# The last projection of a hybrid encoder layer, computed as seven half-size block products instead of eight

## The chip, the cores and the metric

The kernel runs on one core of one Trainium2 chip. The metric is the device time of one execution in microseconds (us). A core has a matrix engine (TensorE; its rows are marked PE, and its weight loads PEld), a vector engine (DVE), an activation engine (ACT) and a general engine (POOL). Each works through its own list of instructions in order, and they wait for each other by semaphores. Transfers between memory and the on-chip buffer are issued here by a fifth engine, SyncE (SP), which also takes its list in order. Matrix products are written into eight PSUM banks; POOL cannot read those, DVE and ACT can.

## The reference

The layer normalises x (512 tokens by 1024 channels), makes one wide input projection, runs two token mixers (a chunked mLSTM and stick-breaking attention), and ends with three projections of 1024 by 1024:

```python
g_m, g_s = split(sigmoid(gates))
merged = g_m * (y_m @ w_proj_m) + g_s * (y_s @ w_proj_s)     # 512 x 1024
x = x + merged @ w_out                                       # 512 x 1024
```

The change concerns the last line only, and what prepares it. All data are float32.

## The kernel before

**Products of split numbers.** Every float32 operand is split into a rounded high part and the rest: `split` (L89 to L91) is one ACT copy for the high part and one DVE subtraction for the low part, which needs the high part. `mm3` (L84 to L87) then makes a product of three matmuls: high by high, high by low, low by high.

**Units.** The dense work is a list of 112 units, and a loop over them (L980) writes the instruction lists of all engines. A unit has a 512 KB block of a weight matrix, loaded by SP into a buffer `stg` (three of them), split into `wh` and `wl` (three of each), and 24 matmuls, each with a moving operand of 512 columns. In step c of the loop the order is: the evacuation of unit c-1 (what DVE and ACT do with its finished PSUM banks), then whatever the table `later` holds for step c, then `ahead(c)` (L973), which issues the split of unit c+2 and the load of unit c+4, then the first half of unit c's matmuls, the steps of the token mixers, and the second half. The order is fixed by hand (`manual_schedule`), so an instruction in an engine's list starts only after those written before it.

**The end of the list.** Units 88 to 95 are the projection of y_s, 96 to 103 the projection of y_m, 104 to 111 the last projection. In the first two a unit makes 128 channels for all 512 tokens; `pm_evac` (L848) evacuates a unit of the y_m projection: `gm = ps * gm` and `gm = gm + gs` on DVE, and a split of gm into `mgh` and `mgl`, the stationary operands of the last projection. The last projection (`tok_group`, L134) goes through two halves of 512 output columns; for each, four units of 256 rows of `w_out` are accumulated into four PSUM banks, one for each block of 128 tokens. After the fourth unit the banks are added to the residual `xr` on DVE, and the sums are stored (L874 to L879). The eight loads of `xr` stand in `later` at unit 104 (L962).

POOL has nothing to do in these last units.

Of the kernel before, what the change touches and what calls it, by code (L numbers as in the profile page):

```python
# [8 lines left out]
F32 = mybir.dt.float32  # L9
FR = mybir.dt.float32r  # L10
BF = mybir.dt.bfloat16
AF = mybir.ActivationFunctionType
OP = mybir.AluOpType

D = 1024
T = 512
KT = 8
TB = 4
# [16 lines left out]
def tile_hybrid_layer(  # L35
# [16 lines left out]
    nc = tc.nc  # L52
    xf = x.flatten_outer_dims()
    of = out.flatten_outer_dims()

    def pool(name, bufs=1, **k):
        return ctx.enter_context(tc.tile_pool(name=name, bufs=bufs, **k))

    cst = pool("cst")
    hp = pool("hp")  # L60
    sp = pool("sp")
    mp = pool("mp")
# [5 lines left out]
    BUFS = {"stg": 3, "wh": 3, "wl": 3, "tmp": 2, "acc": 1, "om": 3, "P5": 2, "A": 4,  # L68
            "qk": 18, "vh": 5, "vl": 5, "y": 16, "brow": 1}
# [3 lines left out]
    def blk(tag, dt=F32, shape=(512,), name=None, p=128):  # L73

        where = mp if tag in MISC else sp
        return where.tile([p] + list(shape), dt, name=name or tag, tag=tag, bufs=BUFS[tag])

    def dense_ps():
        return psd.tile([128, 512], F32, name="dps", tag="dps")
# [4 lines left out]
    def mm3(ps, ah, al, bh, bl, first, last):  # L84
        nc.tensor.matmul(ps, ah, bh, start=first, stop=False)  # L85
        nc.tensor.matmul(ps, ah, bl, start=False, stop=False)  # L86
        nc.tensor.matmul(ps, al, bh, start=False, stop=last)  # L87

    def split(src, hi, lo):  # L89
        nc.scalar.activation(hi, src, AF.Copy)  # L90
        nc.vector.tensor_tensor(lo, src, hi.bitcast(F32), op=OP.subtract)  # L91


    class Unit:


        def __init__(self, src, c0, rows=None):
            if rows is None:
                self.ap = src[:, c0:c0 + 128].rearrange("(k p) c -> p k c", p=128)
                self.shape = [KT, 128]  # L100
            else:
                self.ap = src[rows:rows + 256, c0:c0 + 512].rearrange("(k p) c -> p k c", p=128)
                self.shape = [2, 512]
            self.slow = None
            self.heavy = False

        def load(self, tag="stg"):
            self.st = blk(tag, shape=self.shape)
            nc.sync.dma_start(self.st, self.ap)
# [6 lines left out]
    units = []  # L116

    def chan_group(src, c0, n, mov, evac, slow=None):
        for ct in range(n // 128):
            u = Unit(src, c0 + 128 * ct)  # L120

            def mm(half, u=u, ct=ct):
                if half == 0:
                    u.ps = dense_ps()
                for k in range(4 * half, 4 * half + 4):
                    mh, ml = mov(k)
                    mm3(u.ps, u.wh[:, k, :], u.wl[:, k, :], mh, ml, k == 0, k == KT - 1)

            u.mm = mm
            u.evac = lambda u=u, ct=ct: evac(ct, u.ps)  # L130
            u.slow = slow
            units.append(u)

    def tok_group(src, c0, sta, evac, first=False, b0=None, row=None):  # L134
        ps = [None] * TB
        n0 = len(units)

        def evacs(ps):
            rest = None
            for tb in range(TB):  # L140
                then = evac(tb, ps[tb])
                if rest:
                    rest()
                rest = then
            if rest:
                rest()

        if row is not None:
            later.setdefault(n0 + (0 if first else 2), []).append(lambda: row.append(bias_row(b0)))
        if first:  # L150
            for tb in range(TB):
                u = Unit(src, c0, 256 * tb)
                u.evac = lambda tb=tb: evac(tb, f_ps[tb])
                units.append(u)
            return
        for g in range(4):
            u = Unit(src, c0, 256 * g)

            def mm(half, u=u, g=g):
                for tb in (2 * half, 2 * half + 1):  # L160
                    if g == 0:
                        ps[tb] = dense_ps()
                    for i in range(2):
                        k = 2 * g + i
                        sh, sl = sta(k, tb)
                        mm3(ps[tb], sh, sl, u.wh[:, i, :], u.wl[:, i, :], k == 0, k == KT - 1)

            u.mm = mm
            u.heavy = g == 3
            u.evac = (lambda: evacs(ps)) if g == 3 else (lambda: None)  # L170
            units.append(u)
# [8 lines left out]
    later = {}  # L180
# [75 lines left out]
    hh = hp.tile([128, KT, T], FR, name="hh", tag="hh")  # L256
    hl = hp.tile([128, KT, T], FR, name="hl", tag="hl")
# [37 lines left out]
    def bias_row(c0):  # L295
        b = blk("brow")
        nc.sync.dma_start(b, bass.AP(tensor=b_in.tensor, offset=b_in.offset + c0, ap=[[0, 128], [1, 512]]))
        return b
# [485 lines left out]
    gs_t, gm_t = [], []  # L784
# [42 lines left out]
    def y_late(src, dst, k, at):  # L827
        def run():
            if not big:
                y_big()  # L830
            dst[k] = big["h"][:, at, :], big["l"][:, at, :]
            split_y(src, dst, k)
        return run

    def y_own(k):
        def run():
            ymp[k] = blk("y", FR, name="ymh"), blk("y", FR, name="yml")
            split_y(y_m, ymp, k)
        return run
# [4 lines left out]
    chan_group(w_proj_s, 0, D, lambda k: ysp[k], ps_evac)  # L844

    merged = []

    def pm_evac(ct, ps):  # L848
        g, t = gs_t[ct], gm_t[ct]
        nc.vector.tensor_tensor(t, ps, t, op=OP.mult)  # L850
        nc.vector.tensor_tensor(t, t, g, op=OP.add)
        th = blk("y", FR, name="mgh")
        tl = blk("qk", FR, name="mgl")
        split(t, th, tl)
        merged.append((th, tl))

    chan_group(w_proj_m, 0, D, lambda k: ymp[k], pm_evac)
    n_proj = len(units)

    def m_sta(k, tb):  # L860
        ts = slice(tb * 128, (tb + 1) * 128)
        return merged[k][0][:, ts], merged[k][1][:, ts]

    xr = {}

    def load_xr(g):
        def run():
            xr[g] = [blk("vl" if g else "vh", shape=(512 if g else 576,), name="xr")[:, 0:512] for tb in range(TB)]
            for tb in range(TB):
                nc.sync.dma_start(xr[g][tb], xf[tb * 128:(tb + 1) * 128, g * 512:(g + 1) * 512])  # L870
        return run

    for g in range(2):
        def evac(tb, ps, g=g):  # L874
            t = xr[g][tb]
            n = 256 if g == 1 and tb == TB - 1 else 512
            for c in range(0, 512, n):
                nc.vector.tensor_tensor(t[:, c:c + n], ps[:, c:c + n], t[:, c:c + n], op=OP.add)
                nc.sync.dma_start(of[tb * 128:(tb + 1) * 128, g * 512 + c:g * 512 + c + n], t[:, c:c + n])  # L879

        tok_group(w_out, g * 512, m_sta, evac)


    f_w = []
# [74 lines left out]
    for k in range(8):  # L959
        later.setdefault(n_gates + 3 + k // 2, []).append(  # L960
            y_late(y_m, ymp, k, k) if k < 5 else y_own(k))
    later.setdefault(n_proj, []).append(load_xr(0))  # L962
    later.setdefault(n_proj, []).append(load_xr(1))

    N = len(units)
    count = {"loaded": 4, "ready": 4}
# [13 lines left out]
    for c in range(N):  # L980
# [24 lines left out]
        for e in list(pend):  # L1005
            if c >= e[0] and e[2]():
                pend.remove(e)
                g = e[3]()
# [36 lines left out]
```

## Time and profile before

| what | value |
|---|---|
| median of 3 runs | 719.03 us (718.92 to 719.14) |
| the profiled execution, its own time | 720.13 us |
| its span, from first to last instruction | 718.4 us |
| granted TensorE clock, mean | 0.997 |
| PE busy | 709.8 us (99%) |
| DVE, ACT, POOL busy | 424.5, 315.8, 93.5 us |
| bytes moved | 67.8 MB, 94 GB/s |

How to read it: a row of the timeline gives the start (us from the span's start), the duration, the engine, the line of the kernel, the operation, output and inputs by name, shapes, and a count where rows were merged; square brackets give the idle time in front and what ended it. A row of a list of groups gives a count, then the sum of busy time and the mean of one in ns. A row of a table by stretches gives the busy time of PE, PEld, DVE, ACT and POOL in each stretch with the number of instructions, then the granted clock, the share of the DMA engines and GB/s.

### The profile page before, as it was taken

How to read it: one execution, taken by the hardware profiler on the slowest of the kernel's cores; microseconds unless marked ns; L12 is line 12 of the kernel's file. 1: busy time of each engine (PE TensorE's matmuls, PEld its weight loads, DVE VectorE, ACT ScalarE, POOL GpSimd, SP SyncE). 2: the span in 40 equal slices, each digit the busy share in tenths (PEclk: the TensorE clock that was granted, in tenths of full speed). 3: DMA queues.
4: the chain of work that ended last, by engine and by line, in shares of the span. 5: the costliest groups of instructions: out<-in, count | busy, mean ns of one | idle time of the engine just before them, and what ended most of it. 6: DMA issues, size and time to landing. Idle time of an engine off the chain costs nothing.

```text
span 718.4 us, 9058 instructions
## 1 busy us (share of the span) xinstructions
PE 709.8 (99%) x3356; PEld 593.1 (83%) x3356; DVE 424.5 (59%) x663; ACT 315.8 (44%) x601; POOL 93.5 (13%) x235
## 2 busy tenths in 40 slices
PE   7999999999999999999999999999999999999997
PEld 5888888888888888888888888888888888888886
DVE  5837886656487568279944737994343254556441
ACT  5245364476255544244475534447554343222210
POOL 5422022253022112000001110000112000000000
PEclk9999999999999999999999999999999999999999
DMA  6433332233323222333332233333223333333621
GB/s 239 133 103 81 109 86 77 69 95 92 99 62 87 58 86 62 102 91 97 101 94 59 63 99 88 91 100 89 74 59 89 89 91 97 104 88 89 234 89 58
DMA packets 91475, 67.80 MB, mean 94 GB/s; under 512 B 3470, under 2 KB 77608, under 8 KB 91432
## 3 DMA queue, kind: packets, MB, share of 16 engines
q1 hardware_dynamic: 91432, 67.23, 32.8%
q8 instruction: 26, 0.43, 0.2%
q14 instruction: 17, 0.14, 0.1%
HBM read 65.12 MB, written 2.10 MB: 94 GB/s over the span
## 4 chain that ended last, share of the span: by engine, by line
PE 97%; DMA 1%; DVE 1%; POOL 0%; SPq 0%; issue 0%; ACT 0%; DVEq 0%
PE dps L85 28%; PE dps L87 27%; PE dps L86 27%; PE aps L86 2%; PE aps L87 2%; PE aps L85 2%; PE aps L440 1%; PE aps L382 1%; DMA stg<-in_w_in_dram 1%; PE dps L934 1%; PE dps L932 1%; PE dps L933 1%; PE aps L735 1%; PE aps L736 1%; PE aps L737 1%; DVE fl L891 0%
## 5 line engine op out<-in xcount | busy, mean ns | idle before, releaser
L91 DVE TENSOR_TENSOR wl<-stg,wh 128x1024 fp32r<-128x1024 f32 x108 | 132.3, 1225 | 140.3 <-ACT wh L90 139.9
L85 PE MATMUL dps<-hh,wh 128*128 128x512 f32 x448 | 175.8, 392 | 0.0
L86 PE MATMUL dps<-hl,wh 128*128 128x512 f32 x448 | 174.6, 390 | 0.0
L87 PE MATMUL dps<-hh,wl 128*128 128x512 f32 x448 | 174.6, 390 | 0.0
L90 ACT ACTIVATE wh<-stg 128x1024 fp32r<-128x1024 f32 x108 | 113.6, 1052 | 95.3 <-PE dps L87 58.6
L87 PEld LDWEIGHTS dps<-hh,wl 128*128 128x128 f32 x448 | 84.1, 188 | 17.7
L85 PEld LDWEIGHTS dps<-hh,wh 128*128 128x128 f32 x448 | 84.2, 188 | 17.5 <-issue 1.0
L86 PEld LDWEIGHTS dps<-hl,wh 128*128 128x128 f32 x448 | 84.2, 188 | 16.6
L85 PE MATMUL dps<-wh,hh 128*128 128x512 f32 x224 | 88.3, 394 | 0.0
L87 PE MATMUL dps<-wh,hl 128*128 128x512 f32 x224 | 87.4, 390 | 0.0
L86 PE MATMUL dps<-wl,hh 128*128 128x512 f32 x224 | 87.4, 390 | 0.0
L87 PEld LDWEIGHTS dps<-wh,hl 128*128 128x128 f32 x224 | 42.1, 188 | 8.9
L86 PEld LDWEIGHTS dps<-wl,hh 128*128 128x128 f32 x224 | 42.1, 188 | 8.2
L85 PEld LDWEIGHTS dps<-wh,hh 128*128 128x128 f32 x224 | 42.1, 188 | 8.2
L626 DVE SCALAR_TENSOR_TENSOR acc<-tmp,vec,acc 128x511 f32<-128x511 f32 (+2 forms) x48 | 36.0, 750 | 1.7
L629 ACT ACTIVATE tmp<-acc 128x512 f32<-128x512 f32 x16 | 10.1, 633 | 50.2 <-DVE acc L626 50.2
L415 DVE TENSOR_TENSOR_SCAN om<-om 128x512 f32<-128x512 f32 (+3 forms) x32 | 27.9, 871 | 6.3 <-POOL om L409 6.3
L409 POOL TENSOR_SCALAR_AFFINE_SELECT om<-om 128x128 f32<-128x128 f32 x32 | 12.1, 378 | 134.5 <-ACT om L407 134.5
L90 ACT ACTIVATE at_split<-aps 128x384 fp32r<-128x384 f32 (+1 forms) x24 | 11.8, 525 | 36.8 <-PE aps L440 36.8
L688 POOL TENSOR_SCALAR_AFFINE_SELECT w_all<-om 128x128 f32<-128x128 f32 x16 | 4.1, 293 | 168.9 <-DVE om L683 168.9
L91 DVE TENSOR_TENSOR at_split<-aps,at_split 128x384 fp32r<-128x384 f32 (+1 forms) x24 | 13.7, 599 | 19.8 <-ACT at_split L90 19.8
L86 PE MATMUL dps<-wl,mgh 128*128 128x512 f32 x64 | 24.9, 389 | 0.0
(239 smaller groups left out, 1170.6 us busy)
## 6 DMA issues: line engine op xcount, KB each, us to landing
stg<-in_w_in_dram SPq DMA_DIRECT2D x87, 512.0 KB, 3.7
stg<-in_w_proj_s_dram SPq DMA_DIRECT2D x8, 512.0 KB, 3.7
stg<-in_w_proj_m_dram SPq DMA_DIRECT2D x8, 512.0 KB, 3.6
stg<-in_w_out_dram SPq DMA_DIRECT2D x8, 512.0 KB, 3.7
brow<-in_b_in_dram SPq DMA_DIRECT2D x8, 256.0 KB, 4.2
xr<-in_x_dram SPq DMA_DIRECT2D x8, 256.0 KB, 5.7
out_dram<-xr SPq DMA_DIRECT2D x7, 256.0 KB, 2.3
x<-in_x_dram SPq DMA_DIRECT2D x3, 512.0 KB
```

Of the source, the lines that this page charges most:

```text
L85: nc.tensor.matmul(ps, ah, bh, start=first, stop=False)
L86: nc.tensor.matmul(ps, ah, bl, start=False, stop=False)
L87: nc.tensor.matmul(ps, al, bh, start=False, stop=last)
L90: nc.scalar.activation(hi, src, AF.Copy)
L91: nc.vector.tensor_tensor(lo, src, hi.bitcast(F32), op=OP.subtract)
L382: nc.tensor.transpose(tp[:, tb * 128:(tb + 1) * 128], self.raw[name][tb][:, hs], ident)
L409: nc.gpsimd.affine_select(out=om[:, ts], in_=om[:, ts], compare_op=OP.is_gt, fill=1.0, base=0, channel_multiplier=1, pattern=[[-1, 128]])
L415: nc.vector.tensor_tensor_scan(back, back, back, 1.0, op0=OP.mult, op1=OP.bypass)
L440: nc.tensor.transpose(tp[:, at + (i - j) * 128:at + (i - j + 1) * 128], a_t[i][:, j * 128:(j + 1) * 128], ident)
L626: nc.vector.scalar_tensor_tensor(acc[:, j:], t[:, 0:T - j], cw(3 - j, ch), acc[:, j:], op0=OP.mult, op1=OP.add)
L629: nc.scalar.activation(t, acc, AF.Sigmoid)
L735: nc.tensor.matmul(nm[:, 0:258], ph, vh, start=j == 0, stop=False)
```

## The change

The 512 tokens, 1024 inner channels and 1024 output columns are each cut in half: merged becomes A11, A12 (the first 256 tokens; channel tiles 0 to 3 and 4 to 7) and A21, A22 (the last 256 tokens), and w_out becomes B11, B12, B21, B22. Eight products of such blocks give the result; Winograd's form of Strassen's method needs seven, of sums of blocks:

- S1 = A21 + A22, S2 = S1 - A11, S3 = A11 - A21, S4 = A12 - S2
- T3 = B22 - B12, T2 = B11 + T3, T1 = B22 - T2, T4 = B21 - T2 (the sign taken up in the sums)
- P1 = A11 B11, P2 = A12 B21, P5 = S1 T1, P6 = S2 T2, P7 = S3 T3, P4 = A22 T4, P3 = S4 B22
- the four blocks of the result are sums of these: U = P1 + P6, then U + P7, and so on

A product is two new units (`Product`, g = 0 and 1) of 12 matmuls each, so the eight units 104 to 111 become fourteen, 104 to 117, in the order P1, P2, P6, P5, P7, P4, P3. Beside the matmuls:

- **S1 and S2** are made in `pm_evac` for channel tiles 4 to 7 (steps 101 to 104): two DVE additions of 128x256 and a split of the 128x512 result, behind the split of gm.
- **S3 and S4** (`s34_turn`) are made in steps 105 to 108, one channel tile a step: two DVE subtractions of 128x256 and a split.
- **T1 to T4** are made on POOL, two instructions of 128x1024 each: T3 in steps 100 and 101, T2 in 103 and 104, T1 in 105 and 106, T4 in 107 and 108.
- **Loads**: B22 in steps 96 and 97 and B12 in 98 and 99, by entries of `later`; B11 and B21 with their units; `xr` in step 102.
- **Evacuation**: each product is added to the sums it belongs to when its second unit is done. Those of P1, P2, P5, P4 and P3 are DVE additions that read PSUM (P1 with two ACT copies beside them), P6 and P7 have two such DVE additions and two and four POOL additions of 128x512.

The diff (lines of the old `load_xr` and `m_sta` left out):

```diff
--- before.py
+++ after.py
@@ -844,6 +844,7 @@
     chan_group(w_proj_s, 0, D, lambda k: ysp[k], ps_evac)
 
     merged = []
+    s12 = []
 
     def pm_evac(ct, ps):
         g, t = gs_t[ct], gm_t[ct]
@@ -853,32 +854,176 @@
         tl = blk("qk", FR, name="mgl")
         split(t, th, tl)
         merged.append((th, tl))
+        if ct >= 4:
+            a = gm_t[ct - 4]
+            nc.vector.tensor_tensor(g[:, 0:256], a[:, 256:512], t[:, 256:512], op=OP.add)
+            nc.vector.tensor_tensor(g[:, 256:512], g[:, 0:256], a[:, 0:256], op=OP.subtract)
+            sh, sl = blk("vh", FR, (576,), name="s12h")[:, 0:512], blk("vl", FR, name="s12l")
+            split(g, sh, sl)
+            s12.append((sh, sl))
 
     chan_group(w_proj_m, 0, D, lambda k: ymp[k], pm_evac)
     n_proj = len(units)
 
...
+    s34 = []
+    raw = {}
+    def s34_turn(j):
+        a, t, g = gm_t[j], gm_t[4 + j], gs_t[4 + j]
+        if not s34:
+            s34.append(hp.tile([128, 8, T], FR, name="s34", tag="hh"))
+        nc.vector.tensor_tensor(a[:, 0:256], a[:, 0:256], a[:, 256:512], op=OP.subtract)
+        nc.vector.tensor_tensor(a[:, 256:512], t[:, 0:256], g[:, 256:512], op=OP.subtract)
+        split(a, s34[0][:, j, :], s34[0][:, 4 + j, :])
+    def w_load(name, g, tag):
+        r, c = {"B11": (0, 0), "B12": (0, 512), "B21": (512, 0), "B22": (512, 512)}[name]
+        where = mp if tag == "stg" else sp
+        t = where.tile([128, 2, 512], F32, name=name, tag=tag, bufs=BUFS[tag])
+        nc.sync.dma_start(t, w_out[r + 256 * g:r + 256 * g + 256, c:c + 512].rearrange("(k p) c -> p k c", p=128))
+        raw[name, g] = t
+    def t3(g):
+        d = raw["T3", g] = raw["B12", g]
+        nc.gpsimd.tensor_tensor(d, raw["B22", g], d, op=OP.subtract)
+    def t2(g):
+        d = raw["T2", g] = raw["B11", g]
+        nc.gpsimd.tensor_tensor(d, raw["T3", g], d, op=OP.add)
+    def t1(g):
+        if g == 0:
+            raw["t1"] = hp.tile([128, 4, 512], F32, name="t1", tag="hl")
+        d = raw["T1", g] = raw["t1"][:, 2 * g:2 * g + 2, :]
+        nc.gpsimd.tensor_tensor(d, raw["B22", g], raw["T2", g], op=OP.subtract)
+    def t4(g):
+        d = raw["T4", g] = raw["B21", g]
+        nc.gpsimd.tensor_tensor(d, d, raw["T2", g], op=OP.subtract)
+    def a_sta(k0, t0):
+        return lambda k, tb: [m[:, t0 + 128 * tb:t0 + 128 * tb + 128] for m in merged[k0 + k]]
+    def s_sta(which):
+        o = 256 * ((which - 1) % 2)
+        def sta(k, tb):
+            c = slice(o + 128 * tb, o + 128 * tb + 128)
+            if which <= 2:
+                return s12[k][0][:, c], s12[k][1][:, c]
+            return s34[0][:, k, c], s34[0][:, 4 + k, c]
+        return sta
 
     xr = {}
 
...
+    def load_xr():
+        for n, (g, tb) in enumerate([(0, 0), (0, 1), (1, 0), (1, 1), (1, 2), (1, 3), (0, 2), (0, 3)]):
+            tag = ["om", "om", "om", "acc", "tmp", "tmp", "brow", "vh"][n]
+            t = blk(tag, shape=({"om": 516, "vh": 576}.get(tag, 512),), name="xr")[:, 0:512]
+            nc.sync.dma_start(t, xf[tb * 128:(tb + 1) * 128, g * 512:(g + 1) * 512])
+            xr[g, tb] = t
+    bank = {}
+    class Product:
+        def __init__(self, p, sta, name, g, ps, tag=None, evac=None):
+            self.p, self.sta, self.name, self.g, self.ps, self.tag = p, sta, name, g, ps, tag
+            self.slow = None
+            self.heavy = False
+            self.evac = evac if g else lambda: None
+        def load(self):
+            if self.tag:
+                w_load(self.name, self.g, self.tag)
+        def split(self):
+            self.wh = blk("wh", FR, (2, 512))
+            self.wl = blk("wl", FR, (2, 512))
+            split(raw[self.name, self.g], self.wh, self.wl)
+        def mm(self, tb):
+            if self.g == 0:
+                bank[self.p, tb] = self.ps()
+            for i in range(2):
+                k = 2 * self.g + i
+                sh, sl = self.sta(k, tb)
+                mm3(bank[self.p, tb], sh, sl, self.wh[:, i, :], self.wl[:, i, :], k == 0, k == 3)
+    def add(g, tb, src, store=False, eng=None, n=512):
+        t = xr[g, tb]
+        for c in range(0, 512, n):
+            (eng or nc.vector).tensor_tensor(t[:, c:c + n], src[:, c:c + n], t[:, c:c + n], op=OP.add)
+            if store:
+                nc.sync.dma_start(of[tb * 128:(tb + 1) * 128, g * 512 + c:g * 512 + c + n], t[:, c:c + n])
+    u = []
+    def p1():
+        uu = blk("stg", shape=(2, 512), name="u")
+        for tb in range(2):
+            u.append(uu[:, tb, :])
+            nc.scalar.activation(u[tb], bank[1, tb], AF.Copy)
+            add(0, tb, bank[1, tb])
+    def p2():
+        for tb in range(2):
+            add(0, tb, bank[2, tb], True)
+    def p6():
+        for tb in range(2):
+            nc.vector.tensor_tensor(u[tb], u[tb], bank[6, tb], op=OP.add)
+            add(1, tb, u[tb], eng=nc.gpsimd)
+    def p5():
+        for tb in range(2):
+            add(1, 2 + tb, bank[5, tb])
+            add(1, tb, bank[5, tb])
+    def p7():
+        for tb in range(2):
+            nc.vector.tensor_tensor(u[tb], u[tb], bank[7, tb], op=OP.add)
+            add(0, 2 + tb, u[tb], eng=nc.gpsimd)
+        for tb in range(2):
+            add(1, 2 + tb, u[tb], True, nc.gpsimd)
+    def p4():
+        for tb in range(2):
+            add(0, 2 + tb, bank[4, tb], True)
+    def p3():
+        for tb in range(2):
+            add(1, tb, bank[3, tb], True, n=256 if tb else 512)
+    for p, sta, name, ps, tag, evac in (
+            (1, a_sta(0, 0), "B11", dense_ps, "A", p1),
+            (2, a_sta(4, 0), "B21", dense_ps, "stg", p2),
+            (6, s_sta(2), "T2", att_ps, None, p6),
+            (5, s_sta(1), "T1", att_ps, None, p5),
+            (7, s_sta(3), "T3", dense_ps, None, p7),
+            (4, a_sta(4, 256), "T4", dense_ps, None, p4),
+            (3, s_sta(4), "B22", att_ps, None, p3)):
+        for g in range(2):
+            units.append(Product(p, sta, name, g, ps, tag, evac))
+    def at(c, fn, *a):
+        later.setdefault(n_proj + c, []).append(lambda: fn(*a))
 
     for g in range(2):
-        def evac(tb, ps, g=g):
-            t = xr[g][tb]
-            n = 256 if g == 1 and tb == TB - 1 else 512
-            for c in range(0, 512, n):
-                nc.vector.tensor_tensor(t[:, c:c + n], ps[:, c:c + n], t[:, c:c + n], op=OP.add)
-                nc.sync.dma_start(of[tb * 128:(tb + 1) * 128, g * 512 + c:g * 512 + c + n], t[:, c:c + n])
-
-        tok_group(w_out, g * 512, m_sta, evac)
+        at(-8 + g, w_load, "B22", g, "P5")
+        at(-6 + g, w_load, "B12", g, "A")
+        at(-4 + g, t3, g)
+        at(-1 + g, t2, g)
+        at(1 + g, t1, g)
+        at(3 + g, t4, g)
+    at(-2, load_xr)
+    for j in range(4):
+        at(1 + j, s34_turn, j)
 
 
     f_w = []
@@ -959,8 +1104,6 @@
     for k in range(8):
         later.setdefault(n_gates + 3 + k // 2, []).append(
             y_late(y_m, ymp, k, k) if k < 5 else y_own(k))
-    later.setdefault(n_proj, []).append(load_xr(0))
-    later.setdefault(n_proj, []).append(load_xr(1))
 
     N = len(units)
     count = {"loaded": 4, "ready": 4}
```

More of the change, by code (lines that the diff above doesn't have):

```diff
@@ L855, in pm_evac @@
         merged.append((th, tl))
+        if ct >= 4:
[5 more added lines that the diff above has]
+            s12.append((sh, sl))
     chan_group(w_proj_m, 0, D, lambda k: ymp[k], pm_evac)
     n_proj = len(units)
-    def m_sta(k, tb):
-        ts = slice(tb * 128, (tb + 1) * 128)
-        return merged[k][0][:, ts], merged[k][1][:, ts]
@@ L864, in tile_hybrid_layer @@
-    xr = {}
[L866 to L871, printed above, removed]
-    for g in range(2):
-        def evac(tb, ps, g=g):
-            t = xr[g][tb]
-            n = 256 if g == 1 and tb == TB - 1 else 512
-            for c in range(0, 512, n):
-                nc.vector.tensor_tensor(t[:, c:c + n], ps[:, c:c + n], t[:, c:c + n], op=OP.add)
-                nc.sync.dma_start(of[tb * 128:(tb + 1) * 128, g * 512 + c:g * 512 + c + n], t[:, c:c + n])
-        tok_group(w_out, g * 512, m_sta, evac)
+    s34 = []
```

## The prediction

> **What bounds the kernel now.** I read the page's busy times and its chain of waits first, then the timeline of the matmuls at the end, then a table by stretches of the last stage.
>
> ```profile
> span 718.4 us, 9058 instructions
> PE 709.8 (99%) x3356; PEld 593.1 (83%) x3356; DVE 424.5 (59%) x663; ACT 315.8 (44%) x601; POOL 93.5 (13%) x235
> PE 97%; DMA 1%; DVE 1%; POOL 0%; SPq 0%; issue 0%; ACT 0%; DVEq 0%
> ...
> L86 PE MATMUL dps<-wl,mgh 128*128 128x512 f32 x64 | 24.9, 389 | 0.0
> ...
> 670.48 0.39 PE L85 MATMUL dps<-wh,mgh 128*128 128x512 f32 x1
> ...
> 713.77 0.39 PE L87 MATMUL dps<-wh,mgl 128*128 128x512 f32 x1
> ...
> 670.48:692.24 21.76, 21.76 (x97) 18.03 (x96) 8.87 (x10) 4.76 (x5) 0.00 (x0) 1.00 0.48 164
> ```
>
> PE is the bound, 97% of the chain. The last projection has three groups of 64 matmuls (one row shown, the other two are alike), from 670.48 to the last start at 713.77: 191 spacings in 43.29 us, **0.2267 us a matmul** (the 389 ns of a row overlap the next). A unit of 24 takes 5.44 us, and the stage would end at 714.00. No gap is left, so only fewer matmuls help, and any new wait costs in full. DVE's 59% is an average; what the change asks of DVE falls into steps 101 to 109, and a share says little of a list that is taken in order.
>
> **The matmuls removed.** Seven products of 24 are 168 instead of 192, all again with 512 moving columns: 24 x 0.2267 = **5.44 us less** on PE. A new unit of 12 lasts 2.72 us, and this is the crux: each still needs a split of 128x1024, so the time in which a split must be ready is halved in the very steps in which S1 to S4 are added to the same lists.
>
> **What DVE and ACT do in one step.** The evacuation in step 101 (unit 100's), as it is now, with the rows that give spacings:
>
> ```profile
> 654.36 0.69 DVE L850 TENSOR_TENSOR gm<-dps,gm 128x512 f32<-128x512 f32 x1 [1.15 <-PE dps L87]
> 655.09 0.69 DVE L851 TENSOR_TENSOR gm<-gm,gs 128x512 f32<-128x512 f32 x1
> 655.81 0.63 ACT L90 ACTIVATE mgh<-gm 128x512 fp32r<-128x512 f32 x1 [3.86 <-DVE gm L851]
> 656.35 1.04 ACT L90 ACTIVATE wh<-stg 128x1024 fp32r<-128x1024 f32 x1
> 656.48 0.69 DVE L91 TENSOR_TENSOR mgl<-gm,mgh 128x512 fp32r<-128x512 f32 x1 [0.70 <-ACT mgh L90]
> 657.42 1.23 DVE L91 TENSOR_TENSOR wl<-stg,wh 128x1024 fp32r<-128x1024 f32 x1 [0.26 <-ACT wh L90]
> ...
> 688.09 1.23 DVE L91 TENSOR_TENSOR wl<-stg,wh 128x1024 fp32r<-128x1024 f32 x1 [4.17 <-ACT wh L90]
> 689.24 1.28 DVE L878 TENSOR_TENSOR xr<-dps,xr 128x512 f32<-128x512 f32 x2
> ...
> 714.20 0.76 DVE L878 TENSOR_TENSOR xr<-dps,xr 128x256 f32<-128x256 f32 x2 [0.67 <-PE dps L87]
> ```
>
> From them: an independent 512 operation starts 0.60 after the one before (1.28 - 0.69, rounded), one behind a 1024 operation 1.15 (689.24 - 688.09), a 256 one lasts 0.42 and takes 0.34 when it follows another; an engine that waits for the other goes on 0.04 later. Now a step needs 3.06 + 1.23 = 4.3 us of the 5.44.
>
> *Steps 101 to 104, with S1 and S2.* mgl starts at +2.12; first addition +2.72; second, which needs it, +3.17 to +3.59; ACT's high part of S2's tile +3.63 to +4.26; its low part on DVE +4.30; ACT's wh, next in its list, +4.17; wl 1.07 later at +5.24; the next step's first operation at +5.24 + 1.15 = **+6.40**. That is over 5.44.
>
> *s34_turn and a split.* Two subtractions at 0 and +0.34 (to +0.76), ACT +0.80, its wh +1.34, wl +2.41, next +3.56: **3.56**. *Two PSUM additions* (P1, P2): **1.20**.
>
> DVE's list without any other delay, on the old trace's clock: step 101 at 654.36, 102 at 660.76, 103 at 667.16, 104 at 673.56, 105 at 679.96; 106 at 683.52 (3.56); 107 at 688.28 (1.20 + 3.56); 108 at 691.84; there wl of unit 110 starts at 691.84 + 1.20 + 2.41 = 695.45 and ends at 696.68. PE could have started unit 110 at 670.48 + 6 x 2.72 = 686.80. Its second matmul is the first that reads wl, so it starts effectively at 696.72 - 0.23 = 696.49: **9.7 us of waiting**, over units 106 to 110. From step 109 on DVE has two splits and at most four PSUM additions (2.3 + 2.4 us) in a pair of units of 5.44, and catches up. So 8 x 2.72 = 21.76 us later, at 718.25, the matmuls end, against 714.00: **+4.3 us**, or 9.7 - 5.4.
>
> **POOL beside DVE.** The trace has POOL's two-input operation only at the start, in 128x512:
>
> ```profile
> 9.83 0.68 DVE L288 TENSOR_TENSOR hh<-aps,nw_t 128x512 fp32r<-128x512 f32 x1
> 10.00 2.51 POOL L891 TENSOR_TENSOR fl<-stg,fh 128x512 fp32r<-128x512 f32 x2 [3.96 <-ACT fh L890]
> ...
> 13.76 1.62 POOL L891 TENSOR_TENSOR fl<-P,fh 128x512 fp32r<-128x512 f32 x1 [0.33 <-ACT fh L890]
> 14.14 1.79 DVE L891 TENSOR_TENSOR fl<-stg,fh 128x512 fp32r<-128x512 f32 x1
> ...
> 13.76 3.32 POOL L891 TENSOR_TENSOR fl<-P,fh 128x512 fp32r<-128x512 f32 x2 [0.33 <-ACT fh L890]
> 14.14 3.49 DVE L891 TENSOR_TENSOR fl<-stg,fh 128x512 fp32r<-128x512 f32 x2
> ...
> L891 POOL TENSOR_TENSOR fl<-stg,fh 128x512 fp32r<-128x512 f32 x2 | 2.5, 1274 | 4.0 <-ACT fh L890 4.0
> L747 POOL TENSOR_TENSOR hst<-hst 128x1 f32<-128x1 f32 x16 | 3.3, 209 | 1.3
> ```
>
> At 10.00 POOL ran beside DVE operations that read PSUM: 1274 ns each, DVE's 0.68 unharmed. From 13.76 both engines ran operations with two SBUF inputs, and took turns: DVE's first, 0.69 in the undisturbed row at 655.09, lasted 1.79, from 14.14 to 0.55 after POOL's ended at 15.38; POOL's second ended at 17.08, DVE's second at 17.63, 0.55 behind again. The one that comes second waits for nearly the whole of the other. The rest of the argument takes that for 128x1024 too, where no row shows it.
>
> A POOL operation of 1024: 0.21 + 2 x (1.274 - 0.21) = **2.34** (estimate; bounds 2 x 1.06 = 2.13 and 2 x 1.274 = 2.55). T3 (steps 100, 101) has data early and meets a DVE with 1.1 us a step to spare. The six others fall into DVE's tight stretch. T2 overwrites B11, so it starts when the split of unit 104 (then 105) is done, at the end of step 102 (103): the evacuation's multiplication reads PSUM and goes on, gm + gs, due 0.60 later, waits 1.65, twice. T1's two follow at once in step 104 and hold mgl for 1.44 (the rest of the 2.34 lies in the wait for ACT) and the first S addition for 2.24. T4 overwrites B21 behind the splits of 106 and 107: it holds the second subtraction of step 105 for 2.24, and in step 106, beside P1's two PSUM additions, the next subtraction for 1.16. Sum 1.65 + 1.65 + 1.44 + 2.24 + 2.24 + 1.16 = **10.4 us**, all in front of unit 110's split, hence all on PE. With the bounds for one operation 9.0 to 11.6; if the turn-taking covers only half of an operation of 1024, about 5.
>
> The Trainium skill, SBUF — State Buffer, Who interferes with whom, says the same against this change: an operation of DVE with two SBUF inputs and one of GpSimd (POOL) that reads SBUF exclude each other, and the earlier keeps the port for its whole instruction, whatever its length; by it the 10.4 stand and the 5 does not. GPSIMD Engine Reference, Elementwise — side-by-side cycle accounting, gives 4497 ns for 2048 elements, an estimate of 2.25 for 1024; by it the sum would be some 0.5 us lower.
>
> **The rest, costed at nothing.**
>
> ```profile
> stg<-in_w_out_dram SPq DMA_DIRECT2D x8, 512.0 KB, 3.7
> xr<-in_x_dram SPq DMA_DIRECT2D x8, 256.0 KB, 5.7
> ...
> 664.58 4.06 SPq L870 DMA_DIRECT2D xr<-in_x_dram  x8
> ```
>
> w_out is still eight loads of 512 KB. B22 and B12 stand on SP ahead of the loads of units 100 to 102, B21's load behind eight issues for xr (4.06 us); a load lands 3.7 to 5.7 us after its issue and is wanted two steps, 10.9 us, after. Without that cover B12 would land a step late, and T3 would hold step 101's additions: +1.7. P1's two ACT copies (about 0.7 each) run while ACT waits for DVE. The POOL additions of P6 and P7 come when DVE is ahead. The end is as before: one store of 256 KB, then two of half the size, 718.4 - 714.0 = 4.4 us behind the last matmul.
>
> **Sum.** -5.4 + 9.7 + 10.4 = +14.7. On the profiled execution's 720.13 that is 734.8; this execution stands 1.1 us over the median, so I forecast **733.7** for the median, from 719.03.
>
> **Rivals.**
>
> *The engines work side by side* (chance 0.15). POOL's operations don't hold DVE's, or for a part only. For it: nothing at 1024; against it the rows at 13.76. It leaves +4.3, **723.3**, or up to 728 with half holds.
>
> *DVE keeps up* (0.10), the other side: **713.6**, 719.03 - 5.44. The mechanism: splits run two units ahead, so a late DVE costs nothing until the lead is used up. It decides where wl of unit 110 is ready by 686.80. For it: DVE's busy share, 8.87 of 21.76 us; against it, the list above misses by 9.7 even without POOL. It would need step 101's chain to be shorter than 5.44, or the order in the lists to be other than written. Half of such a gain, no change at all, gets 0.04.
>
> *The clock drops* (0.13). Under my sum PE waits some 9 us before unit 106.
>
> ```profile
> 10.00:15.00 5.00, 4.34 (x12) 3.42 (x13) 4.90 (x12) 4.45 (x8) 4.50 (x5) 0.66 0.85 301
> ...
> 717.00:718.40 1.40, 0.00 (x0) 0.00 (x0) 0.00 (x0) 0.00 (x0) 0.00 (x0) 0.62 0.00 0
> ```
>
> Idle since 714, PE shows a mean granted clock of 0.62 in the last 1.4 us; between 10 and 15 us a mean of 0.66 in five, a loss of 0.34 x 5 = 1.7 us of matmul time. A drop behind the long wait meets units 106 and 107, where PE waits for DVE anyway; it costs something only if one falls on the dense run from unit 110: 733.7 + 1.7 = **735.4**. Against it: the waits before 107 to 110 come out at 1 to 3 us each, with matmuls between them. The Trainium skill, TensorE: Matmul & The Clock Gate, Part 1: The HAM clock gate, puts the drop to half speed at one idle window of about 3.4 us and the return at as long a busy one; by it the 9 us wait drops the clock, and the shorter ones don't. The last rows of the trace agree: the clock falls some 3.3 us behind the last matmul.
>
> **How the numbers follow.** Chances: my sum 0.58, the clock 0.13, side by side 0.15, keeping up 0.10, no change 0.04. Predicted is the likeliest, 733.7. The sum's own range is 732.3 to 736.6 (the bounds of POOL's operation, -1.4 and +1.2, and T3 late, +1.7). The range of 722.8 to 737.5 adds the side-by-side case below and the clock above; only the faster and unchanged cases, 0.14, and a little at the ends lie outside. A run of this kernel tells a change of 0.2%, 1.4 us, from none: faster 0.10, same 0.04, slower 0.86.
>
> **What would show it.** In the changed profile: 168 matmuls in the last projection at 0.227 us; step 101's wl about 5.2 us behind its gm multiplication and step 102's multiplication 6.4 behind that; DVE's gm + gs in steps 103 and 104 at 2.3 us instead of 0.69 while POOL runs; PE idle before units 105 to 110, most before 106, its releaser ACT's wh or DVE's wl, and none after unit 111. A DVE row of 0.69 beside a POOL operation of 2.3 would make the middle term wrong; a PE without gaps from 670 on, all of it.

## The result

The changed kernel takes 736.3 us (median of four runs, 735.1 to 737.2) where the kernel before takes 719.1: a ratio of 1.024, with a 95% interval of 1.0226 to 1.0255. It is 17.2 us slower; 14.7 were forecast, 733.7 us, with a range of 722.8 to 737.5. The profiled execution took 736.70 us, with a span of 735.0.

The page of the changed kernel, its busy times and chain of waits, and then what PE waited for (us in total, times, longest):

```profile
span 735.0 us, 9091 instructions
PE 711.6 (97%) x3332; PEld 591.4 (80%) x3332; DVE 463.5 (63%) x701; ACT 327.5 (45%) x617; POOL 124.6 (17%) x249
PE 93%; DVE 3%; DMA 1%; ACT 1%; issue 1%; POOL 0%; SPq 0%; DVEq 0%; ACTq 0%
...
PE dps L85 <- ACT wh L90: 8.8, 2, 6.2
PE aps L85 <- ACT wh L90: 2.2, 2, 2.0
PE dps L86 <- DVE wl L91: 1.6, 3, 0.8
PE aps L86 <- DVE wl L91: 1.5, 2, 0.8
```

24 matmuls fewer (3332 for 3356), and yet a longer span. PE, which had no gap in this stage, now stands 14.1 us, always for the split of a weight block. Of the 16.6 us between the two spans that and the 5.4 saved leave 7.9. Of these, 5.8 are longer spacings between matmuls with no wait between them, most at a lower clock, while the next split was not ready yet (last section); the rest lies beside the waits, where a matmul alone takes 0.5 to 0.8 us instead of the 0.227 of a dense row of them.

Where the splits are held up is in the timeline of DVE and POOL. Lines 851 and 852 are the two gm operations of `pm_evac`, 860 and 861 the additions for S1 and S2, 880 and 881 those for S3 and S4, 897, 903 and 907 are T2, T1 and T4 on POOL:

```profile
654.45 0.69 DVE L851 TENSOR_TENSOR gm<-dps,gm 128x512 f32<-128x512 f32 x1 [1.15 <-PE dps L87]
659.70 1.23 DVE L91 TENSOR_TENSOR wl<-stg,wh 128x1024 fp32r<-128x1024 f32 x1 [0.26 <-ACT wh L90]
660.85 0.68 DVE L851 TENSOR_TENSOR gm<-dps,gm 128x512 f32<-128x512 f32 x1
667.95 2.44 DVE L852 TENSOR_TENSOR gm<-gm,gs 128x512 f32<-128x512 f32 x1
672.88 0.69 DVE L91 TENSOR_TENSOR mgl<-gm,mgh 128x512 fp32r<-128x512 f32 x1 [2.49 <-PE dps L87]
677.15 0.68 DVE L851 TENSOR_TENSOR gm<-dps,gm 128x512 f32<-128x512 f32 x1
677.87 2.42 DVE L852 TENSOR_TENSOR gm<-gm,gs 128x512 f32<-128x512 f32 x1
680.99 2.08 DVE L91 TENSOR_TENSOR mgl<-gm,mgh 128x512 fp32r<-128x512 f32 x1 [0.70 <-ACT mgh L90]
682.99 2.55 DVE L860 TENSOR_TENSOR gs<-gm 128x256 f32<-128x256 f32 x1
689.24 2.47 DVE L881 TENSOR_TENSOR gm<-gm,gs 128x256 f32<-128x256 f32 x1
695.70 1.65 DVE L880 TENSOR_TENSOR gm<-gm 128x256 f32<-128x256 f32 x1
707.98 2.36 DVE L91 TENSOR_TENSOR wl<-t,wh 128x1024 fp32r<-128x1024 f32 x2 [0.25 <-ACT wh L90]
...
667.45 2.40 POOL L897 TENSOR_TENSOR B<-B,B 128x1024 f32<-128x1024 f32 x1 [20.19 <-DVE wl L91]
677.37 2.37 POOL L897 TENSOR_TENSOR B<-B,B 128x1024 f32<-128x1024 f32 x1 [7.53 <-issue]
679.70 5.57 POOL L903 TENSOR_TENSOR t<-B,B 128x1024 f32<-128x1024 f32 x2
688.95 2.48 POOL L907 TENSOR_TENSOR B<-B,B 128x1024 f32<-128x1024 f32 x1 [3.69 <-DVE wl L91]
694.66 2.40 POOL L907 TENSOR_TENSOR B<-B,B 128x1024 f32<-128x1024 f32 x1 [3.23 <-DVE wl L91]
```

Three things are to be seen. The first three rows give the chain of step 101: wl 5.25 us behind the gm multiplication, the next step's multiplication 6.40 behind it, which is more than the 5.44 of a unit. Then, each time POOL has an operation under way, one DVE operation of 0.69 or 0.42 lasts 1.65 to 2.55, and ends 0.3 to 0.6 us behind POOL's. And at 672.88 DVE comes out of a wait that PE ended: that one was not in the forecast. Everything behind it in DVE's list, up to unit 110's wl at 707.98, is later by it.

### The profile page after: what moved, and what is told of

It is laid out like the page before. It is cut to its first block, busy times and chain, and to the rows that moved or that the text cites. A ratio compares the mean times of both kernels' runs of the same rounds, so it can differ in the third digit from the quotient of the medians.

```text
span 735.0 us, 9091 instructions
## 1 busy us (share of the span) xinstructions
PE 711.6 (97%) x3332; PEld 591.4 (80%) x3332; DVE 463.5 (63%) x701; ACT 327.5 (45%) x617; POOL 124.6 (17%) x249
## 3 DMA queue, kind: packets, MB, share of 16 engines
HBM read 65.12 MB, written 2.10 MB: 91 GB/s over the span
## 4 chain that ended last, share of the span: by engine, by line
PE 93%; DVE 3%; DMA 1%; ACT 1%; issue 1%; POOL 0%; SPq 0%; DVEq 0%; ACTq 0%
PE dps L85 25%; PE dps L87 25%; PE dps L86 25%; PE aps L86 3%; PE aps L87 3%; PE aps L85 3%; PE aps L440 1%; PE aps L382 1%; DMA stg<-in_w_in_dram 1%; PE dps L1079 1%; DVE wl L91 1%; PE dps L1077 1%; PE dps L1078 1%; ACT wh L90 1%; PE aps L735 1%; PE aps L736 1%
## 5 line engine op out<-in xcount | busy, mean ns | idle before, releaser
L91 DVE TENSOR_TENSOR wl<-stg,wh 128x1024 fp32r<-128x1024 f32 x100 | 124.4, 1244 | 123.9 <-ACT wh L90 123.8
L90 ACT ACTIVATE wh<-stg 128x1024 fp32r<-128x1024 f32 x100 | 105.2, 1052 | 75.4 <-PE dps L87 41.2
L85 PE MATMUL dps<-yh,wh 128*128 128x512 f32 x64 | 24.9, 389 | 0.0
```

## The experiments

The kernel before was run beside each group: 719.06 us beside the first four, 719.39 beside the last four.

| kernel | time, us | ratio to the kernel before, 95% |
|---|---|---|
| changed kernel | 736.29 | 1.0226 to 1.0255 |
| without T1 to T4 | 726.96 | 1.0100 to 1.0134 |
| mgl of two tiles in other buffers | 733.50 | 1.0189 to 1.0219 |
| both | 723.18 | 1.0049 to 1.0080 |
| T1 to T4 as memsets | 728.67 | 1.0114 to 1.0144 |
| without any sums | 713.22 | 0.9900 to 0.9930 |
| without T1 to T4, new order | 713.61 | 0.9907 to 0.9940 |
| T1 to T4 on POOL, new order | 724.25 | 1.0055 to 1.0086 |
| T1 to T4 by ACT and DMA, new order | 714.03 | 0.9913 to 0.9943 |

A whole execution also holds what comes ahead of step 101, where these edits change nothing but T3, and that differs by over a microsecond from one profiled execution to another (see the end of the next section). Within the stage the profiles compare closely. The table has, for the changed kernel and the four runs in the old order with S1 to S4, the start of step 101's gm multiplication, the start of unit 110's wl, the time between the two, and the time from there to the end of the span, all in us. The prediction's list puts 41.1 between the two without POOL (695.45 - 654.36), and 51.5 with its 10.4.

| kernel | step 101 | wl of unit 110 | between | to the end |
|---|---|---|---|---|
| changed kernel | 654.45 | 707.98 | 53.5 | 27.0 |
| without T1 to T4 | 652.98 | 697.98 | 45.0 | 27.0 |
| mgl of two tiles in other buffers | 653.18 | 704.91 | 51.7 | 27.0 |
| both | 653.22 | 694.69 | 41.5 | 28.6 |
| T1 to T4 as memsets | 653.39 | 698.39 | 45.0 | 28.6 |

### Without T1 to T4

```diff
-        d = raw["T2", g] = raw["B11", g]
-        nc.gpsimd.tensor_tensor(d, raw["T3", g], d, op=OP.add)
+        raw["T2", g] = raw["B11", g]
...
```

(and the same for T1, T3 and T4)

> T1 to T4 are left out: POOL's eight operations of 128x1024 are gone and P6, P5, P7 and P4 take the raw blocks B11, B22, B12 and B21 in their place (the sums differ, all other work is the same). Theory: POOL's operations hold DVE's operations with two SBUF inputs, and DVE's list sets when unit 110 can start. Then DVE's rows lose their waits: gm + gs in steps 103 and 104 at 0.69 us instead of 2.44 and 2.42, and wl of unit 110 starts 8.9 us earlier (699.0 instead of 707.98, counted on from step 104 at 677.15, which stays because mgl of step 103 still waits for PE until 672.88). Time 727.4. Rival, DVE's list is long by itself and POOL costs nothing: 736.3.

726.96 us. DVE's steps 103 and 104 in this kernel:

```profile
666.48 0.69 DVE L852 TENSOR_TENSOR gm<-gm,gs 128x512 f32<-128x512 f32 x1
671.41 0.69 DVE L91 TENSOR_TENSOR mgl<-gm,mgh 128x512 fp32r<-128x512 f32 x1 [4.23 <-PE dps L87]
676.40 0.69 DVE L852 TENSOR_TENSOR gm<-gm,gs 128x512 f32<-128x512 f32 x1
```

Without POOL's operations the rows are at 0.69 again, and 9.3 us are gone, of the 8.9 expected. Within the stage it is 8.5 (53.5 - 45.0), which is what the five holds behind step 103 add up to by the changed kernel's rows (1.73 + 1.39 + 2.13 + 2.05 + 1.23). The wait that PE ends has grown from 2.49 to 4.23: its end is fixed by PE, so what POOL had cost in step 103 now goes into it.

### The two low parts in other buffers

```diff
-        tl = blk("qk", FR, name="mgl")
+        tl = blk("y" if ct > 5 else "qk", FR, name="mgl")
```

> The low parts mgl of channel tiles 6 and 7 get buffers of another tag (y, which has two left) instead of the 18 of tag qk, of which 20 are wanted at once. Theory: the 2.49 us in which DVE stands before mgl in step 103, ended by PE, is the wait for the buffer that unit 104 reads; without it mgl starts at 671.0 instead of 672.88 and all that follows comes 1.9 us earlier: 734.4. Rival, the wait is covered elsewhere or has another cause: 736.3, with the idle time still there.

733.50 us, 2.8 us less (1.9 expected), and the wait is ACT's again:

```profile
653.18 0.69 DVE L851 TENSOR_TENSOR gm<-dps,gm 128x512 f32<-128x512 f32 x1 [1.15 <-PE dps L87]
666.68 2.44 DVE L852 TENSOR_TENSOR gm<-gm,gs 128x512 f32<-128x512 f32 x1
669.82 0.69 DVE L91 TENSOR_TENSOR mgl<-gm,mgh 128x512 fp32r<-128x512 f32 x1 [0.70 <-ACT mgh L90]
704.91 2.36 DVE L91 TENSOR_TENSOR wl<-t,wh 128x1024 fp32r<-128x1024 f32 x2 [0.26 <-ACT wh L90]
```

Within the stage the gain is 1.8 us (53.5 - 51.7), as expected; the rest of the 2.8 is not the buffer's: of the 3.1 us between the two spans (735.0 and 731.9), 1.3 lie ahead of step 101 (654.45 and 653.18). So the new wait is one for a buffer. The tag qk has 18. The change keeps eight gm and four gs tiles until S3 and S4 are made, which leaves six for the eight mgl; before, gm tiles came free as soon as they were split. By the time at which the wait ends, the seventh mgl takes the buffer of the first, which unit 104 reads.

### Both

The two edits together.

> Both: T1 to T4 left out as in the run without them, and mgl of tiles 6 and 7 in other buffers. Theory: only DVE's own list remains, 6.40 us a step in 101 to 104 and 3.56 or 4.76 a step behind, which by the sum on record costs 9.7 us of PE's time against 5.4 saved: 723.4, still slower than 719.1. Rival, without POOL DVE keeps up: 713.7.

723.18 us, 4.1 over the kernel before (interval 3.5 to 5.8), against 723.4 expected from DVE's list alone. With POOL gone and the buffers there, the seven products still lose. The difference between this run and the one before it is POOL's share with nothing else in it: 733.50 - 723.18 = 10.3 us, and within the stage 10.3 as well (51.7 - 41.5, before rounding 51.73 - 41.47):

```profile
653.22 0.69 DVE L851 TENSOR_TENSOR gm<-dps,gm 128x512 f32<-128x512 f32 x1 [1.15 <-PE dps L87]
694.69 2.36 DVE L91 TENSOR_TENSOR wl<-B,wh 128x1024 fp32r<-128x1024 f32 x2 [0.25 <-ACT wh L90]
```

### T1 to T4 as memsets

```diff
-        nc.gpsimd.tensor_tensor(d, raw["T3", g], d, op=OP.add)
+        for c in (0, 1, 0, 1, 0):
+            nc.gpsimd.memset(d[:, c, :], 0.0)
```

(and the same in the other three)

> POOL's eight T operations are replaced by memsets of the same buffers, five of 128x512 each (some 2.5 us, about as long as one operation of 2.4), so that T1 to T4 are zero: the order, the buffers and what waits for POOL's results stay, only POOL reads nothing from SBUF. Theory, the two engines exclude each other where POOL reads: DVE's rows are at 0.69 again and the time is that of the run without T, 727.4. Rival, the time goes in waiting for T's values or in POOL being busy at all: 736.3.

728.67 us; its interval overlaps that of the run without T (726.96). POOL's groups, and DVE's gm + gs of steps 103 and 104:

```profile
L899 POOL MEMSET B<- 128x512 f32 x10 | 4.8, 527 | 30.3 <-DVE wl L91 30.3
L906 POOL MEMSET t<- 128x512 f32 x10 | 4.7, 528 | 0.0
L911 POOL MEMSET B<- 128x512 f32 x10 | 4.8, 526 | 0.6 <-DVE wl L91 0.6
...
666.90 0.69 DVE L852 TENSOR_TENSOR gm<-gm,gs 128x512 f32<-128x512 f32 x1
676.81 0.69 DVE L852 TENSOR_TENSOR gm<-gm,gs 128x512 f32<-128x512 f32 x1
```

POOL is as busy as with T1, T2 and T4 (14.3 us against 15.2), in the same buffers and the same order, and DVE's rows are undisturbed. Within the stage the run takes 45.0 us to unit 110's wl, as the run without T does; the 1.7 us between their medians are matched by what the profiled execution loses behind that wl (28.6 us to the end instead of 27.0), where the clock fell (last section). So it is neither POOL being busy nor the wait for T's values that costs 9 to 10 us, but POOL's reading of the buffer beside DVE operations with two inputs there. The Trainium skill, SBUF — State Buffer, Who interferes with whom, says both: contention with a POOL instruction that reads, none with one that only writes. The two runs agree.

### Without any sums

T1 to T4 as raw blocks, no S3 and S4, and in `pm_evac`:

```diff
-            nc.vector.tensor_tensor(g[:, 0:256], a[:, 256:512], t[:, 256:512], op=OP.add)
-            nc.vector.tensor_tensor(g[:, 256:512], g[:, 0:256], a[:, 0:256], op=OP.subtract)
...
-            split(g, sh, sl)
-            s12.append((sh, sl))
+            s12.append((th, tl))
```

> All sums in front of the products are left out, S1 to S4 and T1 to T4: the seven products take raw blocks of merged and w_out. The fourteen units, their splits, loads and evacuations stay. Theory: with the additions gone DVE needs 4.3 us a step as before and 1.15 to 2.35 us (3.6 once, in step 112) a half-size step of 2.72, so PE has no gap and what is left is the 24 matmuls saved: 719.1 - 5.4 = 713.7. Rival, units of half the size don't keep PE fed because each still needs a whole split: over 716.

713.22 us, 6.2 less than the kernel before (interval 5.0 to 7.2), 713.7 expected. Fourteen units of half the size feed PE without a gap in this stage. The 24 matmuls are worth what was counted.

### A new order in DVE's and ACT's lists, without T1 to T4

```diff
+            nc.scalar.activation(th, t, AF.Copy)
             nc.vector.tensor_tensor(g[:, 0:256], a[:, 256:512], t[:, 256:512], op=OP.add)
             nc.vector.tensor_tensor(g[:, 256:512], g[:, 0:256], a[:, 0:256], op=OP.subtract)
...
+            nc.scalar.activation(sh, g, AF.Copy)
+            nc.vector.tensor_tensor(tl, t, th.bitcast(F32), op=OP.subtract)
+            nc.vector.tensor_tensor(sl, g, sh.bitcast(F32), op=OP.subtract)
...
-        at(1 + j, s34_turn, j)
+        at((3, 3, 5, 5)[j], s34_turn, j)
+        at((4, 5, 7, 7)[j], s34_split, j)
```

> T1 to T4 are left out as before (raw blocks in their place), S1 to S4 are all made. Besides, mgl of tiles 6 and 7 in buffers of tag y, the two S additions of a step put in front of the low parts, so that DVE makes them while ACT makes the high part, and the S3 and S4 work moved from steps 105 to 108 to steps 107 to 111. Theory: what is left after the run without T and with other mgl buffers (723.2) is DVE standing before ACT; a step of 101 to 104 then needs 6.40 - 1.28 = 5.12 us, under 5.44, and the time is 714 to 715. Rival, DVE's work itself is too much, wherever it stands: 721 to 723.

713.61 us. The same operations, each as long as before, but 9.6 us less than in the run without T and with the other mgl buffers. DVE's steps 101 and 102:

```profile
653.64 0.69 DVE L852 TENSOR_TENSOR gm<-gm,gs 128x512 f32<-128x512 f32 x1
654.37 0.43 DVE L861 TENSOR_TENSOR gs<-gm 128x256 f32<-128x256 f32 x1
654.83 0.43 DVE L862 TENSOR_TENSOR gs<-gs,gm 128x256 f32<-128x256 f32 x1
655.17 0.68 DVE L865 TENSOR_TENSOR mgl<-gm,mgh 128x512 fp32r<-128x512 f32 x1
...
658.35 0.69 DVE L851 TENSOR_TENSOR gm<-dps,gm 128x512 f32<-128x512 f32 x1 [0.22 <-PE dps L87]
```

The additions stand where DVE had waited 0.70 for ACT, the second wait of 0.70 is gone too, and the next step's first operation waits 0.22 for PE again: a step is done within the 5.44 us of its unit. What had made DVE's list too long was its waits for ACT and the place of the S3 and S4 work, not the work. This one run moves both, so what each is worth is not shown.

### The new order with T1 to T4 on POOL

The order and the buffers of the last run, with T1 to T4 on POOL as in the change.

> The same order and buffers as in the run with the new order, but T1 to T4 made on POOL as in the changed kernel, so that all is computed. Theory: POOL's six late operations still hold DVE, for about 10 us in all, of which the time now free in DVE's list takes a part: by the same list 724 (720 to 728). Rival, with the new order there is room enough: 714 to 715.

724.25 us (724 expected), 10.6 over the run without T. By the rows of its trace six operations are held for 10.5 us in all, in step 104 three in a row. Next to nothing of that is absorbed, and the run without T shows why: in this order DVE waits for PE only some 0.22 us a step in steps 102 to 104, and from 673.22 to 704.56 it is busy for 31.19 of 31.34 us.

```profile
671.45 2.45 DVE L852 TENSOR_TENSOR gm<-gm,gs 128x512 f32<-128x512 f32 x1
673.93 2.48 DVE L861 TENSOR_TENSOR gs<-gm 128x256 f32<-128x256 f32 x1
676.45 2.44 DVE L862 TENSOR_TENSOR gs<-gs,gm 128x256 f32<-128x256 f32 x1
```

### T1 to T4 by ACT and adding DMAs

```diff
+    def t_add(name, g, block):
+        nc.gpsimd.dma_start(raw[name, g], w_src(block, g), accum_op=OP.add)
...
+    def t_neg(name, g, block):
+        t = raw[name, g]
+        nc.scalar.activation(t, t, AF.Copy, scale=-1.0)
+        t_add(name, g, block)
...
+        t = raw["T2", g] = sp.tile([128, 2, 512], F32, name="T2", tag="P5", bufs=BUFS["P5"])
+        nc.scalar.activation(t, raw["T3", g], AF.Copy)
+        t_add("T2", g, "B11")
...
```

(T4 likewise, from T2 with scale -1 and B21; T3 starts from B12 and T1 from B11, loaded by SP)

> Everything is computed, with the new order and buffers, and T1 to T4 made without POOL's arithmetic: T3 = -B12 + B22, T2 = T3 + B11, T1 = -B11 + B12, T4 = -T2 + B21, each by one ACT copy of 128x1024 (scale -1 where there is a minus) and one DMA that adds a block of w_out into the buffer; B11, B21 and B22 are loaded for P1, P2 and P3 as ordinary units, so 4 MB more are read. T3 and T2 are made in steps 88 to 94, T1 in 98 to 102, T4 in 105 to 108. Theory: DVE has no POOL reads against it before P6, ACT and the DMA queues have room, so the time is that of the run without T in this order: 714 to 715, faster than the kernel before. Rival, the adding DMAs land late or ACT's eight more copies delay wh: 717 or more.

714.03 us, all computed: 0.7% under the kernel before (ratio 0.9913 to 0.9943). Its page, PE's waits in this stage, the issues and the bytes read:

```profile
span 712.4 us, 9110 instructions
PE 703.8 (99%) x3332; PEld 586.8 (82%) x3332; DVE 450.4 (63%) x701; ACT 335.7 (47%) x625; POOL 114.2 (16%) x249
...
PE dps L86 <- DVE wl L91: 0.5, 1, 0.5
...
stg<-in_w_in_dram SPq DMA_DIRECT2D x87, 512.0 KB, 3.7
T<-in_w_out_dram POOLq DMA_DIRECT2D x6, 512.0 KB, 7.1
...
HBM read 70.37 MB, written 2.10 MB: 102 GB/s over the span
```

PE waits 0.5 us in all in this stage. 70.37 MB are read where the changed kernel reads 65.12, 5.3 more and not the 4 that the expectation counted: 18 transfers of 512 KB from w_out instead of 8, so ten more and not eight. The adding DMAs of T1 to T3 land 7.1 us after their issue (median of six), the loads of w_in 3.7, and no wait of PE, DVE or ACT in this stage ends with one of them. This is the form in which the seven products pay: 5.4 us, about what 24 matmuls are worth.

## Why the prediction was right, point by point

**The matmuls removed (-5.4).** Right: with no sums in front of them, -6.2 us (5.0 to 7.2).

**DVE's own list (+9.7, so +4.3 net).** Right: the run with POOL's operations and the buffer wait taken away is at +4.1. The steps came out as worked out, 5.25 to wl and 6.40 to the next step, where 5.24 and 6.40 stood. A step with S3 and S4 takes 3.66 us (700.60 to 704.26 in the changed kernel), where 3.56 stood; four of them make the 41.5 us of the table out of the 41.1 of the list.

**POOL beside DVE (+10.4).** Right, to within 0.2 us for each operation. 1.65, 1.65, 1.44, 2.24, 2.24 and 1.16 us were worked out; measured against the undisturbed 0.69 and 0.42 are 2.44 - 0.69 = 1.75, 1.73, 1.39, 2.13, 2.05 and 1.23, together 10.3, and 10.3 between the two runs that differ in POOL alone. What the rows before the change could not show, that an operation of 1024 holds DVE for its whole length, is so: the operation was estimated at 2.34 and lasts 2.37 to 2.48. T1's two take 5.57 together, longer than two alone; that DVE's operations hold POOL's in turn would fit, but no run shows it apart. T3 cost nothing, as said, though it ran earlier than the steps in which it stands, in POOL's list: its two operations meet a wl at 635.75 (3.15 us) and an mgl at 645.69 (2.12), and by step 101 DVE is on time again (654.45, 654.36 in the kernel before).

**The edits costed at nothing.** This step failed in one place. It went through queues, loads and PSUM, but not through the buffers: the S sums keep twelve tiles of tag qk alive for longer, and the seventh mgl has to wait for PE to have read the first. In the trace that puts step 104 at 677.15 where the list with POOL's first hold says 675.2 (673.56 + 1.65), 1.9 us; with and without the edit unit 110's wl differs by 1.8 within the stage. With it the sum is 14.7 + 1.8 = 16.5; the two profiled executions are 16.6 apart (735.0 and 718.4), the medians 17.2. So the forecast of 733.7 was 2.6 us short, 1.8 of it by this wait and the rest within the spread of the executions.

**The rivals.** *Side by side* fell with the rows of 2.4 us. *DVE keeps up* fell, but the run with a new order shows how near it was: DVE's busy share was a sign that there was room, only not in that order. *The clock drops* came true, without its price in the changed kernel's profiled execution and with it in those of two experiments: see below. PE's waits stand where they were expected, none behind unit 110, but the longest, before unit 106, is 6.2 us and not some 9: the buffer wait and the low clock had put unit 105 later. In the run with other buffers, where unit 105 waits for 0.79 us, it is 7.6. Loads, xr, P1's copies and the end of the kernel cost nothing, as said; the last matmul starts at 730.68 and the span ends 4.3 us behind that, against 4.6 in the kernel before (713.77 and 718.4).

What the runs leave open: the changed kernel's times spread over 2.1 us, those of the kernel before over 0.2 in the four executions beside it and over 1.2 in the seven beside the last four experiments. The traces show two things that go with it. Between 10 and 15 us the mean granted clock is 0.66 in the profiled executions of the kernel before and of the changed kernel and 1.00 in those of the eight experiments, and step 101 starts at 654.4 in the first two and at 652.9 to 653.4 in the others. And in two executions PE lost 1.6 us behind unit 110 (last section). Which of the executions without a profile had either is not known. So a microsecond or two between the medians of two kernels says less than the rows within the stage.

## What to carry to other kernels

When matmuls are traded for additions, lay the additions into each engine's list in order, with their waits for other engines, and compare step by step with the time that PE now leaves; a busy share of 40% didn't keep this list from being 9.7 us late, and with POOL's operations gone a change of order alone made up for it. POOL arithmetic on buffers is not free parallel work beside DVE operations with two buffer inputs: price each POOL operation as if DVE did it, or make the sum by an ACT copy and an adding DMA, beside which DVE's operations kept their length here. And look for every tile that a change keeps alive longer, counted against the buffers of its tag.

## What was not expected of the hardware

The clock fell after shorter waits than forecast. Matmuls of the changed kernel behind the wait before unit 108 and at unit 110, the stretch of all its waits (columns as in the tables by stretches before), and a stretch behind unit 110 in the run with both edits:

```profile
699.48 0.51 PE L85 MATMUL aps<-wh,s12h 128*128 128x512 f32 x1 [2.00 <-ACT wh L90]
700.73 0.74 PE L86 MATMUL aps<-wl,s12h 128*128 128x512 f32 x1 [0.75 <-DVE wl L91]
701.70 0.63 PE L85 MATMUL aps<-wh,s12h 128*128 128x512 f32 x1
702.13 0.63 PE L86 MATMUL aps<-wl,s12h 128*128 128x512 f32 x1
...
708.00 0.50 PE L85 MATMUL aps<-wh,s12h 128*128 128x512 f32 x1 [0.15 <-ACT wh L90]
...
673.20:708.00 34.80, 21.55 (x63) 14.90 (x61) 28.16 (x32) 11.12 (x16) 12.79 (x5) 0.75 0.04 15
...
696.79:699.78 2.99, 2.99 (x9) 2.30 (x8) 2.99 (x4) 0.00 (x0) 2.05 (x2) 0.50 0.03 8
```

From 701.70 to 702.13 the spacing is 0.43 us instead of 0.227. Before that there had been 2.00 us of waiting, a single matmul and 0.75 more, which the prediction, by the rule it goes by, took to be too little; here the trace decides. The same spacing stands behind the waits before unit 105 (2.58 and 0.76 us) and unit 106 (6.17 and 0.46); the mean granted clock from 673.2 to 708 is 0.75. In this execution it cost nothing visible: from 672.88 to 707.98 no wait of DVE or ACT is ended by PE, so their lists ran on without it, and the matmuls of unit 109 still were done 0.15 us before the split of unit 110 was ready.

In two other executions it had the price that the rival names. In the run with both edits nine matmuls behind unit 110 had a granted clock of 0.50 (last row), in the run with memsets nine had 0.52, and from unit 110's wl to the end both took 28.6 us instead of 27.0: 1.6 us, where the prediction said 1.7. The first of the two executions is the slowest of its four (724.98 us; the others 723.07 to 723.27). These are the dense units, in which nothing else is waited for. In the run with both edits the waits just before were 0.77 and 0.76 us; a like pair before unit 105 in the run with other buffers (0.79 and 0.77) was followed by matmuls at full speed. What decides between the two is not shown.
